# Low parts of table tiles made on VectorE in the gate stage of a decoder layer, and an index row made earlier

## The chip, the cores and the metric

The kernel runs on one core of a Trainium2 chip. What counts is the device time of one execution in microseconds (us), as the median of several runs. The engines are named as in the profile: PE (TensorE, matmuls; PEld its weight loads), DVE (VectorE), ACT (ScalarE), POOL (GpSimd) and SP (SyncE, which issues most DMA transfers). Each engine works through its own queue in order.

## The reference

One layer of a decoder: a norm with scale and shift, a mixer of two attention groups with a residual, a second such norm, and a feed-forward part that picks 16 of 16384 single-neuron experts for each of 8 heads. 512 tokens, width 2048, all in float32. The change touches the last part alone, here shortened:

```python
def peer_ffn(h, w_q, sub_keys, u_tab, v_tab):
    q = (h @ w_q).reshape(B, S, 8, 2, 128)
    s = einsum('bshpd,hpkd->bshpk', q, sub_keys)      # 2 x 128 scores per head
    top_s, top_i = lax.top_k(s, 16)
    cand = top_s[..., 0, :, None] + top_s[..., 1, None, :]
    best_s, best_c = lax.top_k(cand.reshape(..., 256), 16)
    i1 = take_along_axis(top_i[..., 0, :], best_c // 16)
    i2 = take_along_axis(top_i[..., 1, :], best_c % 16)
    expert = i1 * 128 + i2                             # of 128 x 128
    gate = softmax(best_s)
    act = gelu(einsum('td,ted->te', x, u_tab[expert])) # 128 experts per token
    return einsum('te,ted->td', gate * act, v_tab[expert])
```

## The kernel before

The kernel treats 160 tokens sparsely (it gathers rows of the two tables for them by DMA) and the other 352 (`NT`) densely: for these it multiplies with the whole tables u and v and weighs the result with a gate that is zero for experts not picked.

**Products in two parts.** Matmuls with table tiles keep float32 accuracy by splitting both operands. For a half tile of 128 x 1024 weights, `load_w` issues the load of `wraw` on SP, and `split` lets ACT cast it to the high part `whi` (L115) and another engine subtract to get the low part `wlo` (L117); the argument `lo_eng` says which. `whi` and `wlo` have three buffers each, `wraw` has four. `product1(j)` makes one of 128 tiles of u times the tokens: for each of two tile halves 16 matmuls on `whi` (L844) and 8 on `wlo` (L847). It yields between the high and the low part of a half, so that its pieces can be spread among other work. Then ACT takes the gelu (L850). `product2` multiplies with v in the same way (casts L1074, low parts on DVE L1075, matmuls L1080).

**The stages that matter here**, in time: (1) the second stage with the queries, whose weights `w_q` have their low parts on POOL, while DVE picks the top 16; (2) the transposes of the picked indices and gates to `slot` and `gres` (L898 to L906); (3) the gate stage, about 1106 to 1277 us; (4) what is left of the first tiles of u; (5) the long stage of `product2` and further `product1` pieces, with the gathers of the sparse tokens on POOL, to the end.

**The gate stage** builds for each dense token the 128 x 128 table of gates. It runs over 44 groups of 8 tokens. For each group DVE makes four one-hot operations on 128 x 1024 float16: two compares of the index row `iota` with the indices, `o1` (L955) and `o2` (L956), and two products of `o2` with the gates' two parts, `o3` (L960). PE then multiplies `o1` and `o3` token by token (16 table matmuls L967 a group, tile `b_gg`), ACT copies them to `stg` (L970), and SP stores `stg` to DRAM for every 32 tokens. `o1` and `o3` have two buffers, `o2` has one. Between the groups, `next(pieces)` puts one piece of `product1`, so two groups have one tile half between them. 20 tiles of u are made ahead of the fifth stage; 17 of these belong to `product1_pieces`, 34 tile halves, and all have their low parts on POOL.

**The index row** `iota2` is made by POOL (L932), at the head of the gate stage's pool of tiles `ggen`, behind the DMAs of indices and gates (L891, L892) on POOL's queue.

**What follows.** The stored gates come back as `gtile` (four tiles of u at a time, L1051), and `gate()` multiplies the products with them on DVE (L1061), lets ACT cast (L1064) and DVE subtract (L1065). The gathers on POOL (L995) wait for a cast of `product2`.

The order of instructions on each engine is set by a scheduler that goes by the program's order, its dependencies and free buffers; only some are tied by hand (`after`).

## Time and profile before

| what | value |
|---|---|
| median of 3 runs | 3183.56 us (3181.09 to 3184.69) |
| the profiled execution: own time, span | 3180.52 us, 3178.8 us |
| PE busy, share of the span | 3046.1 us, 96% |
| DVE busy | 2585.9 us, 81% |
| ACT busy | 1113.1 us, 35% |
| POOL busy | 937.5 us, 29% |
| low parts on POOL (L117), all forms | x211, 368.7 us |

The times of instructions come from the one profiled execution; the median comes from other runs of the same kernel. A share of busy time is a mean over stages that are limited by different things, so what the change meets is read from its own stage: which engine idles there, and for whom. "Idle before" an instruction is time in which its engine did nothing, and the releaser is what ended it. A matmul's duration overlaps with that of the next; the spacing of their starts tells the pace.

### The profile page before, as it was taken

What the parts mean: (1) busy time and instruction counts of PE and PEld (TensorE: products, weight loads), DVE (VectorE), ACT (ScalarE), POOL (GpSimd) and SP (SyncE); (2) the same over time, 40 slices, a digit from 0 to 9 for tenths busy, and PEclk for the clock granted to TensorE, in tenths of its full rate; (3) what the DMA queues carried; (4) which work ended last, traced back from release to release, by engine and by line L of the source; (5) the groups of instructions that cost most, each with busy time, mean ns of one, the idle gap of its engine ahead of it and who ended that gap; (6) DMA issues with size and microseconds to landing.
All of it is one profiled execution on the core that took longest, in us unless ns stands there. A gap on an engine that the chain in (4) does not pass through costs nothing.

```text
span 3178.8 us, 46249 instructions
## 1 busy us (share of the span) xinstructions
PE 3046.1 (96%) x17617; PEld 2811.5 (88%) x17617; DVE 2585.9 (81%) x3642; ACT 1113.1 (35%) x1604; POOL 937.5 (29%) x630
## 2 busy tenths in 40 slices
PE   3989999999999988999999999999999999999997
PEld 2777777677777877999999999999999999999997
DVE  8988866677589999588888888888888888888885
ACT  3333345432332444433333333333333333333333
POOL 6445430111233433422222222222222222222210
PEclk9999999999999999999999999999999999999999
DMA  7876842148622256899999999999999999999973
GB/s 227 273 237 210 295 157 86 36 145 284 218 93 83 81 193 230 288 339 338 346 332 337 341 340 342 335 351 334 333 348 335 340 336 344 338 346 337 351 297 125
DMA packets 268528, 850.03 MB, mean 267 GB/s; under 512 B 25768, under 2 KB 99528, under 8 KB 224560
## 3 DMA queue, kind: packets, MB, share of 16 engines
q1 hardware_dynamic: 221712, 511.38, 46.8%
q0 software_dynamic: 46592, 335.68, 28.1%
q8 instruction: 138, 2.26, 0.3%
q14 instruction: 86, 0.70, 0.1%
HBM read 814.74 MB, written 32.19 MB: 266 GB/s over the span
## 4 chain that ended last, share of the span: by engine, by line
PE 77%; DVE 15%; DMA 4%; issue 3%; ACT 1%; POOL 0%; SPq 0%; ACTq 0%; DVEq 0%; POOLq 0%
PE b_p L1080 30%; PE b_p L844 19%; PE b_p L847 9%; PE b_o L703 3%; DVE o L960 3%; DMA adaw<-in_ada_w 2%; PE b_pj L109 2%; PE b_pj L110 2%; PE b_pj L108 2%; DVE acc L228 2%; DVE o L955 1%; PE b_o L108 1%; PE b_o L109 1%; PE b_o L110 1%; DVE o L956 1%
## 5 line engine op out<-in xcount | busy, mean ns | idle before, releaser
L115 ACT CAST whi<-wraw 128x1024 fp32r<-128x1024 f32 (+2 forms) x459 | 413.9, 904 | 1032.6 <-PE b_p L844 307.7
L844 PE MATMUL b_p<-h2hi,whi 128*128 128x352 f32 x2048 | 672.4, 329 | 0.0
L844 PE MATMUL b_p<-h2lo,whi 128*128 128x352 f32 x2048 | 667.2, 326 | 0.0
L1080 PE MATMUL b_p<-h2hi,whi 128*128 128x352 f32 x2048 | 655.3, 323 | 1.5 <-DVE xo L1092 0.8
L1080 PE MATMUL b_p<-h2lo,whi 128*128 128x352 f32 x2048 | 653.8, 322 | 0.0
L117 POOL TENSOR_TENSOR wlo<-wraw,whi 128x512 fp32r<-128x512 f32 (+3 forms) x211 | 368.7, 1755 | 460.9 <-ACT whi L115 333.6
L1074 ACT CAST whi<-wraw 128x1024 fp32r<-128x1024 f32 x256 | 268.6, 1049 | 642.8 <-PE b_p L1080 317.3
L1075 DVE TENSOR_TENSOR wlo<-wraw,whi 128x1024 fp32r<-128x1024 f32 x256 | 313.3, 1225 | 161.6 <-ACT whi L1074 138.3
L844 PEld LDWEIGHTS b_p<-h2lo,whi 128*128 128x128 f32 x2048 | 386.6, 189 | 0.1
L844 PEld LDWEIGHTS b_p<-h2hi,whi 128*128 128x128 f32 x2048 | 386.4, 189 | 0.1
L1080 PEld LDWEIGHTS b_p<-h2hi,whi 128*128 128x128 f32 x2048 | 384.4, 188 | 2.4 <-DVE xo L1092 1.1
L1080 PEld LDWEIGHTS b_p<-h2lo,whi 128*128 128x128 f32 x2048 | 384.9, 188 | 0.0
L228 DVE SCALAR_TENSOR_TENSOR acc<-adaw,cact,acc 128x512 f32<-128x512 f32 (+1 forms) x390 | 357.5, 936 | 29.4 <-DMA adaw<-in_ada_w 23.8
L847 PE MATMUL b_p<-h2hi,wlo 128*128 128x352 f32 x2048 | 377.6, 327 | 0.6 <-POOL wlo L117 0.6
L1080 PE MATMUL b_p<-h2hi,wlo 128*128 128x352 f32 x2048 | 369.7, 322 | 0.0
L117 DVE TENSOR_TENSOR wlo<-wraw,whi 128x1024 fp32r<-128x1024 f32 x248 | 304.3, 1227 | 56.0 <-ACT whi L115 53.2
L995 POOL DMA_INDIRECT gat<-in_u_rows,eidx x128 | 195.7, 1529 | 502.8 <-ACT whi L1074 192.2
L847 PEld LDWEIGHTS b_p<-h2hi,wlo 128*128 128x128 f32 x2048 | 339.1, 188 | 0.9 <-POOL wlo L117 0.9
L995 POOL DMA_INDIRECT gat<-in_v_rows,eidx x128 | 185.8, 1451 | 515.7 <-ACT whi L1074 245.2
L1080 PEld LDWEIGHTS b_p<-h2hi,wlo 128*128 128x128 f32 x2048 | 334.0, 188 | 0.0
L1014 DVE SCALAR_TENSOR_TENSOR h2sb<-gat,wt,h2sb 128x2048 f32<-128x2048 f32 x127 | 298.3, 2349 | 24.8 <-DMA gat<-in_v_rows,eidx 24.2
L1001 DVE SCALAR_TENSOR_TENSOR gat<-gat,h2s 128x2048 f32<-128x2048 f32 x128 | 290.8, 2287 | 18.9 <-DMA gat<-in_u_rows,eidx 18.8
(375 smaller groups left out, 4264.5 us busy)
## 6 DMA issues: line engine op xcount, KB each, us to landing
wraw<-in_u_t SPq DMA_DIRECT2D x256, 512.0 KB
wraw<-in_v_t SPq DMA_DIRECT2D x256, 512.0 KB
adaw<-in_ada_w SPq DMA_DIRECT2D x288, 256.0 KB
adaw<-in_ada_w SPq DMA_DIRECT2D x128, 192.0 KB
gd<-stg SPq DMA_DIRECT2D x11, 2048.0 KB
gtile<-gd SPq DMA_DIRECT2D x32, 704.0 KB
wraw<-in_w_out SPq DMA_DIRECT2D x32, 512.0 KB
wraw<-in_w_q SPq DMA_DIRECT2D x32, 512.0 KB
```

The source lines that it names most:

```text
L108: mm(o, wh, xh, start=first, stop=False)
L115: nc.scalar.copy(out=hi, in_=src)
L117: last_lo[0] = e.tensor_tensor(out=lo, in0=src, in1=hi, op=OP.subtract).ins.name
L228: nc.vector.scalar_tensor_tensor(out=acc, in0=w[:, j, :], scalar=cact[:, k:k + 1], in1=acc, op0=OP.mult, op1=OP.add)
L844: mm(b3, uh[:, kk, :], x[:, GA:, k0 + kk, :], start=k0 + kk == 0 and x is h2[0], stop=False)
L847: mm(b3, ul[:, kk, :], h2[0][:, GA:, k0 + kk, :], start=False, stop=k0 + kk == KD - 1)
L995: ins = nc.gpsimd.indirect_dma_start(out=g, out_offset=None, in_=a[table], in_offset=bass.IndirectOffsetOnAxis(ap=idx[:, c:c + 1], axis=0))
L1001: after(nc.vector.scalar_tensor_tensor(out=g, in0=g, scalar=1.0, in1=of(s, h2s, h2sb)[0], op0=OP.mult, op1=OP.mult, accum_out=act0[:, s:s ...
L1014: ins = nc.vector.scalar_tensor_tensor(out=acc, in0=g, scalar=wt0[:, s:s + 1], in1=acc, op0=OP.mult, op1=OP.add)
L1074: pace[0] = nc.scalar.copy(out=vh, in_=vr).ins.name
L1075: pace[1] = nc.vector.tensor_tensor(out=vl, in0=vr, in1=vh, op=OP.subtract).ins.name
L1080: mm(banks[dc][:, :NT], part[:, jj, dc * P:(dc + 1) * P], x, start=first and jj == 0 and part is vh and x is wpair[pair * 2 + jj][0], stop ...
```

## The change

`product1_pieces` asks for its low parts from "vector" instead of "gpsimd": 34 subtractions of 128 x 1024 move from POOL to DVE. And the index row moves out of the pool `ggen` to the pool `slp`, beside the tile `slot`, and is written ahead of the transposes.

```diff
     slot = slp.tile([P, 4, NT], F16, name="slot")
+    iota2 = slp.tile([P, P, 2], F16, name="iota")
+    nc.gpsimd.iota(iota2, pattern=[[1, P], [0, 2]], base=0, channel_multiplier=0,
+                   allow_small_or_imprecise_dtypes=True)
     gres = slp.tile([P, NT], F32, name="gres")
...
     shp = [P, OB // 2, P, 2]
-    iota2 = gg.tile([P, P, 2], F16, name="iota", bufs=1)
-    nc.gpsimd.iota(iota2, pattern=[[1, P], [0, 2]], base=0, channel_multiplier=0,
-                   allow_small_or_imprecise_dtypes=True)
     iota = iota2.unsqueeze(1).broadcast_to(shp)
...
         while done1[0] < RAW + NHOST:
-            yield from product1(next(todo1), "gpsimd")
+            yield from product1(next(todo1), "vector")
             done1[0] += 1
```

Three lines are added ahead of the gate stage and three taken away in it, so lines from L895 to L933 have a number three higher in the changed kernel than before.

Where the instructions go, in the order in which they stand on their engines. A number behind a tile's name tells one buffer's use from another.

DVE at the start of the gate stage, before:

```order
L888 COPY gate0_5825<-gates_7457 128x128
L955 TENSOR_TENSOR o1_9663<-iota_9596,slot_9495 128x1024
L956 TENSOR_TENSOR o2_9664<-iota_9596,slot_9495 128x1024
L905 CAST slot_9495<-gres_9496 128x352
L955 TENSOR_TENSOR o1_9714<-iota_9596,slot_9495 128x1024
L906 TENSOR_TENSOR slot_9495<-gres_9496,slot_9495 128x352
L960 TENSOR_TENSOR o3_9667<-o2_9664,slot_9495 128x1024
L960 TENSOR_TENSOR o3_9669<-o2_9664,slot_9495 128x1024
```

and now:

```order
L888 COPY gate0_5825<-gates_7457 128x128
L955 TENSOR_TENSOR o1_9663<-iota_9496,slot_9495 128x1024
L956 TENSOR_TENSOR o2_9664<-iota_9496,slot_9495 128x1024
L908 CAST slot_9495<-gres_9498 128x352
L117 TENSOR_TENSOR wlo_9604<-wraw_9601,whi_9603 128x1024
L909 TENSOR_TENSOR slot_9495<-gres_9498,slot_9495 128x352
L960 TENSOR_TENSOR o3_9667<-o2_9664,slot_9495 128x1024
L117 TENSOR_TENSOR wlo_9634<-wraw_9631,whi_9633 128x1024
L960 TENSOR_TENSOR o3_9669<-o2_9664,slot_9495 128x1024
```

Two low parts now stand among the first products, and the compare of the second group has gone behind them.

POOL at the same place and to the end of stage 4, a piece of the difference (- before, + now):

```order
 L891 DMA eidxb<-eflat 32x32
 L892 DMA gateb<-gates 32x32
-L932 IOTA iota 128x256
-L117 TENSOR_TENSOR wlo<-wraw,whi 128x1024 x27
 L987 MEMSET accb 128x2048
-L117 TENSOR_TENSOR wlo<-wraw,whi 128x1024 x7
 L995 DMA gat<-in_u_rows,eidxb 128x2048 x16
```

POOL now has nothing between the index DMAs and the gathers but the memset; the index row stands 33 low parts earlier, behind the small index row of the second stage (L760).

DVE in the middle of the gate stage, before:

```order
L956 TENSOR_TENSOR o2_10372<-iota_9596,slot_9495 128x1024
L955 TENSOR_TENSOR o1_10371<-iota_9596,slot_9495 128x1024
L960 TENSOR_TENSOR o3_10375<-o2_10372,slot_9495 128x1024
L960 TENSOR_TENSOR o3_10377<-o2_10372,slot_9495 128x1024
L956 TENSOR_TENSOR o2_10424<-iota_9596,slot_9495 128x1024
L960 TENSOR_TENSOR o3_10427<-o2_10424,slot_9495 128x1024
L955 TENSOR_TENSOR o1_10423<-iota_9596,slot_9495 128x1024
L960 TENSOR_TENSOR o3_10429<-o2_10424,slot_9495 128x1024
```

and now:

```order
L955 TENSOR_TENSOR o1_10371<-iota_9496,slot_9495 128x1024
L956 TENSOR_TENSOR o2_10372<-iota_9496,slot_9495 128x1024
L960 TENSOR_TENSOR o3_10375<-o2_10372,slot_9495 128x1024
L960 TENSOR_TENSOR o3_10377<-o2_10372,slot_9495 128x1024
L955 TENSOR_TENSOR o1_10423<-iota_9496,slot_9495 128x1024
L956 TENSOR_TENSOR o2_10424<-iota_9496,slot_9495 128x1024
L117 TENSOR_TENSOR wlo_10582<-wraw_10579,whi_10581 128x1024
L960 TENSOR_TENSOR o3_10427<-o2_10424,slot_9495 128x1024
L960 TENSOR_TENSOR o3_10429<-o2_10424,slot_9495 128x1024
```

Every second group has a low part between its compares and its products. On PE, around the same place, where the order is that of before:

```order
L847 MATMUL b_p1_10222<-h2hi_7290,wlo_10312 128x352 x8
L967 LDWEIGHTS o1_10371
L967 MATMUL b_gg_10379<-o3_10375,o1_10371 128x128
L967 LDWEIGHTS o1_10371
L967 MATMUL b_gg_10379<-o3_10377,o1_10371 128x128
```

The matmuls on the low part `wlo_10312`, three uses of the buffers before `wlo_10582`, stand ahead of the table matmuls of group 10371.

DVE after the last group of the gate stage, now (before, the gate multiplications followed the last product without a low part among them):

```order
L960 TENSOR_TENSOR o3_11583<-o2_11578,slot_9495 128x1024
L117 TENSOR_TENSOR wlo_11691<-wraw_11688,whi_11690 128x1024
L117 TENSOR_TENSOR wlo_11721<-wraw_11718,whi_11720 128x1024
L117 TENSOR_TENSOR wlo_11754<-wraw_11751,whi_11753 128x1024
L117 TENSOR_TENSOR wlo_11784<-wraw_11781,whi_11783 128x1024
L1061 TENSOR_TENSOR xo_7449<-xo_7449,gtile_12001 128x352
L117 TENSOR_TENSOR wlo_11817<-wraw_11814,whi_11816 128x1024
L1065 TENSOR_TENSOR h2lo_7291<-xo_7449,h2hi_7290 128x352
L1061 TENSOR_TENSOR xo_7449<-xo_7449,gtile_12001 128x352 x3
L1065 TENSOR_TENSOR h2lo_7291<-xo_7449,h2hi_7290 128x352
L1061 TENSOR_TENSOR xo_7449<-xo_7449,gtile_12003 128x352
L117 TENSOR_TENSOR wlo_11847<-wraw_11844,whi_11846 128x1024
```

Four low parts stand ahead of the first gate multiplication and six among those that follow.

## Rows read from the trace of the kernel before

**Rows 1.** Page, part 4: the chain's shares of the span by engine.

```profile
PE 77%; DVE 15%; DMA 4%; issue 3%; ACT 1%; POOL 0%; SPq 0%; ACTq 0%; DVEq 0%; POOLq 0%
```

**Rows 2.** Windows: start:end, length, busy us (x instructions) per engine, PEclk, DMA, GB/s.

```profile
1122.00:1127.00 5.00, 5.00 (x25) 5.00 (x24) 4.58 (x7) 1.20 (x2) 0.00 (x0) 0.54 0.00 0
1143.00:1259.00 116.00, 101.87 (x896) 91.05 (x894) 113.29 (x128) 55.12 (x88) 46.80 (x17) 1.00 0.62 225
1277.00:1321.00 44.00, 43.41 (x275) 43.02 (x274) 20.60 (x28) 20.81 (x32) 29.05 (x12) 1.00 0.78 249
1350.00:1400.00 50.00, 50.00 (x314) 50.00 (x314) 42.75 (x47) 17.85 (x24) 11.89 (x10) 1.00 0.92 339
```

**Rows 3.** Timeline of DVE, mid-stage: start, us, instruction, count [idle before <-releaser].

```profile
1150.30 2.69 DVE L960 TENSOR_TENSOR o<-o,slot 128x1024 f16<-128x1024 f16 x1
1152.91 0.68 DVE L955 TENSOR_TENSOR o<-iota,slot 128x1024 f16<-128x1024 f16 x1
1153.51 0.68 DVE L960 TENSOR_TENSOR o<-o,slot 128x1024 f16<-128x1024 f16 x1
...
1157.55 2.70 DVE L960 TENSOR_TENSOR o<-o,slot 128x1024 f16<-128x1024 f16 x1
```

**Rows 4.** Timeline of POOL at the same time.

```profile
1149.50 2.93 POOL L117 TENSOR_TENSOR wlo<-wraw,whi 128x1024 fp32r<-128x1024 f32 x1 [4.32 <-PE b_p L847]
```

**Rows 5.** Chain of waits, 1260 to 1285: start, us, engine, tile, line, count.

```profile
1271.71 0.94 PE b_gg L967 x16
1272.64 2.68 PE b_p L844 x16
...
1276.25 1.36 PE b_p L847 x8
```

**Rows 6.** Groups by form, 1106 to 1276: count, busy us, mean ns, idle before.

```profile
L117 POOL TENSOR_TENSOR wlo<-wraw,whi 128x1024 fp32r<-128x1024 f32 x24 | 67.1, 2804 | 88.2 <-PE b_p L847 83.9 <-ACT stg L970 4.3
```

**Rows 7.** Timeline of DVE after the stage: a low part, and what follows.

```profile
1329.11 1.23 DVE L1075 TENSOR_TENSOR wlo<-wraw,whi 128x1024 fp32r<-128x1024 f32 x1 [1.91 <-PE b_p L1080]
1330.26 2.28 DVE L1001 SCALAR_TENSOR_TENSOR gat<-gat,h2sb 128x2048 f32<-128x2048 f32 x1
```

**Rows 8.** Timeline of POOL at the stage's start.

```profile
1104.54 1.54 POOL L932 IOTA iota<- 128x256 f16 x1
1106.03 9.39 POOL L117 TENSOR_TENSOR wlo<-wraw,whi 128x1024 fp32r<-128x1024 f32 x4
1116.46 2.34 POOL L117 TENSOR_TENSOR wlo<-wraw,whi 128x1024 fp32r<-128x1024 f32 x1 [1.04 <-PE b_p L847]
```

**Rows 9.** Timeline of DVE at the stage's start.

```profile
1106.11 9.86 DVE L955 TENSOR_TENSOR o<-iota,slot 128x1024 f16<-128x1024 f16 x1 [4.97 <-POOL iota L932]
...
1116.50 2.50 DVE L905 CAST slot<-gres 128x352 f16<-128x352 f32 x1
```

**Rows 10.** Timeline of ACT at the stage's start.

```profile
1104.64 0.28 ACT L902 ACTIVATE gres<-b_sk 128x128 f32<-128x128 f32 x1
```

**Rows 11.** Timeline of PE at the stage's start.

```profile
1115.84 0.49 PE L847 MATMUL b_p<-h2hi,wlo 128*128 128x352 f32 x2
...
1121.29 1.76 PE L967 MATMUL b_gg<-o,o 128*128 128x128 f16 x15 [0.31 <-DVE o L960]
...
1123.25 0.49 PE L844 MATMUL b_p<-h2lo,whi 128*128 128x352 f32 x1
1123.54 0.49 PE L844 MATMUL b_p<-h2hi,whi 128*128 128x352 f32 x1
```

**Rows 12.** Timeline of PE after the stage, low-part matmuls L847.

```profile
1299.34 1.47 PE L847 MATMUL b_p<-h2hi,wlo 128*128 128x352 f32 x8
...
1308.00 1.58 PE L847 MATMUL b_p<-h2hi,wlo 128*128 128x352 f32 x8 [0.58 <-POOL wlo L117]
```

**Rows 13.** Timeline of DVE after the stage, the first gate multiplications.

```profile
1295.14 1.40 DVE L1061 TENSOR_TENSOR xo<-xo,gtile 128x352 f32<-128x352 f32 x3 [21.49 <-DMA gtile<-gd]
```

**Rows 14.** Timeline of POOL in the second stage, behind the sixteen-wide index row.

```profile
896.52 4.71 POOL L117 TENSOR_TENSOR wlo<-wraw,whi 128x1024 fp32r<-128x1024 f32 x2 [4.88 <-ACT whi L115]
```

## The prediction, made before the changed kernel ran

> **What bounds the kernel now.** I read the chain of waits first. It runs over PE for 77% of the span, so nearly everywhere only less idle time on PE pays; DVE has 15% [rows 1]. Then the windows by stage, to find where PE idles: in 1350 to 1400 us, after the gate stage, PE is busy for 50.00 of 50 us, while in 1143 to 1259, the middle of the gate stage, it is busy for 101.87 of 116 and DVE for 113.29 [rows 2]. So in the gate stage DVE sets the pace, and the reader is to see why in DVE's timeline beside POOL's. One period (two groups of 8 tokens) has eight one-hot operations and lasts 1157.55 - 1150.30 = 7.25 us. Seven of them follow each other after 0.6 to 0.8 us; the one that starts at 1150.30 takes 2.69 and the next starts 2.61 later [rows 3]. At that moment POOL makes a low part, from 1149.50 to 1152.43 [rows 4]. There are 17 such low parts in 1143 to 1259 [rows 2] and 17 such long operations on DVE, one in each period, never two and never without POOL. The trace thus shows DVE held until POOL is done. The hold is 2.61 less the usual 0.60 [rows 3] = 2.01 us.
>
> PE's own need in a period is seen at the end of the stage, where the chain runs over PE: 0.94 for each of two groups of table matmuls, 2.68 for the high part of a tile half and 1.36 for its low part, 5.92 us [rows 5]. So PE waits 1.33 us in each period of 7.25.
>
> **The steady part of the stage.** Of the 34 low parts that change engine, 24 lie in the gate stage [rows 6]; five of them come in a heap at the start [rows 8], which leaves 19 in the steady part. What each costs DVE: a low part of the same shape on DVE takes 1.23 us, and the next operation starts 1330.26 - 1329.11 = 1.15 later [rows 7]; I take 1.15, since it is the same instruction between the same engines' work, with 1.40 as the upper bound (a seam of 0.1 to 0.2 on both sides, as between some one-hot operations in [rows 3]). The hold of 2.01 goes, since POOL then has nothing left in the stage but its queue of gathers behind the memset. A period becomes 7.25 - 2.01 + 1.15 = 6.39, still above PE's 5.92, so DVE stays the bound and all of it counts: 19 x 0.86 = **16.3 us**. With 1.40 it is 11.6.
>
> Does a low part make DVE wait? It writes one of three buffers, so it needs the low-part matmuls of the tile half three before. In the order, the low part 10582 stands behind the products 10375 and 10377; the matmuls that free its buffer, those on 10312 (10404 and 10490 have the two other buffers), stand on PE in front of the table matmuls that wait for these very products. When PE waits for DVE, they are long done. The operand whi is cast by ACT, busy for 55.12 of 116 us in that stretch [rows 2]; POOL today starts its low part when PE releases the buffer, not when ACT delivers [rows 4]. I price the wait at nothing.
>
> **The start of the stage.** Today DVE waits 4.97 us for the index row [rows 9], made on POOL from 1104.54 after the index DMAs [rows 8]; then four low parts run on POOL in a row, 9.39 us, and DVE's first compare takes 9.86; the cast behind it takes 2.50, beside the fifth low part [rows 8, 9]. PE has done what stands in front of its first table matmuls at 1115.84 + 0.49 = 1116.3 and gets going at 1121.29 [rows 11]. After the change the index row is long there, and two compares run before ACT delivers the gates at 1104.64 + 0.28 = 1104.9 [rows 10]. Behind that stand the cast, a low part, a subtraction, a product, a low part, a product: 0.5 + 1.15 + 0.5 + 0.6 + 1.15 + 0.6 = 4.5, done at 1109.4 (the cast alone isn't in the trace; between 0.3, half the 0.68 of a compare, and its 2.50 [rows 9], I take 0.5, near to the compares, which have more elements; even 2.50 gives 1111.4). PE then runs from 1116.3 without a pause: 1121.3 - 1116.3 = **5.0 us**. The pause also has a price behind it: in 1122 to 1127, after PE had stood still, the granted clock is 0.54, near the lower of its two levels, 1.2 of 2.4 GHz [rows 2], and matmuls start 0.29 us apart [rows 11] where the same block later takes 2.68 / 16 = 0.17 [rows 5]. 13 of them are so spaced, 13 x 0.12 = **1.6 us**, which should go. Bounds for the two: 3 us, if PE waits for the second group, and 6.6 whole.
>
> **The index row** moves past 33 low parts on POOL's queue, to a place in front of the second stage's low parts, and takes 1.54 us there [rows 8]. POOL sits idle there for 4.88 us before its next low part [rows 14], which waits for ACT; it is hidden, price nothing. Without that cover it would delay one low part by 1.5.
>
> **After the gate stage** ten low parts move. Today PE waits 0.58 us for one of POOL's at 1308.00 [rows 12]: **0.6 us**. In exchange six of the ten stand on DVE behind gate multiplications (L1061) that wait for the gate tiles; the first lands at 1295.14 [rows 13], 19 us after the last table matmuls, which end at 1276.25 [rows 5]. Four low parts stand ahead of them, enough for four tile halves; the fifth is needed by PE at 1299.3 [rows 12] and would be done at 1295.1 + 0.5 + 1.15 = 1296.8. 2.5 us to spare, price nothing; DVE is busy for only 20.60 of 44 us there [rows 2]. The gathers that are now next in POOL's queue wait for ACT's first cast of the following stage, as today, so they don't come forward into this stretch by more than some us.
>
> **The sum** is 16.3 + 5.0 + 1.6 + 0.6 = 23.5 us against the profiled execution's 3180.52 (span 3178.8, with 1.7 around it that nothing touches): 3157.0. The median of the runs stands 3.04 above that execution, so the forecast for the median is 3183.56 - 23.5 = **3160.1 us**. What comes behind is bound by PE at 50.00 of 50 us [rows 2], so a gain made here should stay.
>
> **Rival 1, PE becomes the bound.** If DVE gets ahead at the start and stays there, the stage lasts what PE needs: from 1116.3, 44 groups of 0.94 and 22 tile halves of 4.04 [rows 5] are 130.2 us, to 1246.5 instead of 1276.25. That is 29.7 + 0.6 = 30.3 us: 3153.3. For it: DVE has the first two groups done before PE wants them. Against it: 6.39 against 5.92 in each period. Chance 0.13.
>
> **Rival 2, given back after the stage.** If the gate tiles land later against the end of the stage than today (their stores and loads share the queues with weights), low parts 5 to 10 are late by what exceeds 2.5 us, and PE waits. To leave less than 6 us of gain the landing must slip by 20 us. Against it: the order of the DMA issues is the same in both kernels and the share of the DMA engines is 0.78 there [rows 2]. Chance 0.07 for a result within 0.2%, about 3180.
>
> **Rival 3, slower: the low part waits in DVE's queue.** If a low part reached the head before its buffer is free, the period would be a circle: table matmuls 0.94, high part 2.68, 0.94, low part on PE 1.36, its making on DVE 1.15, two products 1.2, together 8.3 us against 7.25. 19 x 1.0 more, less the 7.2 of start and end: 3195. It decides where PE's low-part matmuls on the freed buffer stands behind the table matmuls that wait for products queued after the low part; the order has it ahead, by one group. Chance 0.03.
>
> **Rival 4, slower: DVE simply has more to do.** If the long operations are not POOL's doing, nothing goes away and each of 19 periods grows by 1.15, 21.9 us, less the 5.0 of the index row: about 3200. Against it: 17 long operations beside 17 low parts, and the 9.86 beside four. Chance 0.04. The Trainium skill, "Perfetto Trace Analysis", section "Optimizing Scalar/DVE Operations", says that offloading from a saturated DVE, even to GpSimd, may make sense; this change does the reverse on a DVE that is busy for 113.29 of 116 us, so by that rule alone one lands here. The same section adds that the two share a read port and that offloading between them might not help; the rows above bear out this half.
>
> **How the numbers follow.** The forecast has 0.73, rival 1 0.13, rival 2 0.07, rivals 3 and 4 together 0.07. Low end: rival 1, and 1 us for the scatter of the runs, 3152. High end: 11.6 + 3 in place of 16.3 + 6.6, no 0.6, gives 3169; with 1 us of scatter, 3170. About 0.2% (6 us) is what can be told from no change here. Faster 0.86, within it 0.07, slower 0.07.
>
> **What would show it.** In the trace of after: no POOL low part after 1103 us, no one-hot operation over 1 us, periods of about 6.4 us on DVE with a low part of 1.2 in each; PE's first table matmuls at about 1116 and the granted clock of the next 5 us near 1; the last table matmuls about 1253 instead of 1276; no PE wait over 1 us for a low part between there and the next stage. Periods of 8 with DVE waiting for PE in front of a low part show rival 3, periods above 8 with long one-hot operations rival 4, and a PE that waits for DVE's low parts after the stage rival 2.

## The result and the profile after

The kernel after takes 3150.86 us in the median of four runs (3147.20 to 3154.82), the kernel before 3182.32 on the same chip; the ratio is 0.9897, with a 95% interval of 0.9880 to 0.9913. The gain of 31 us is larger than the forecast's 23.5 and larger than the 30.3 of its first rival; the time lies 1.1 us under the low end of the range.

The profiled execution of after took 3154.82 us (span 3153.1), which is 25.7 less than that of before. It understates the gain, since something ahead of the stage differs between executions: in all profiles of this study the copy of the first gates (DVE, L888), the last step ahead of the gate stage, starts somewhere between 1097 and 1110 us. In before it starts at 1100.92, in after at 1106.56. The difference of 5.64 us is there before the moved index row can play a part: the small index row of the second stage (L760), which in both kernels stands ahead of it, starts at 891.34 and 896.98, and from there to the copy it is 209.58 us in both. All stage lengths below are therefore counted from that copy; first its line in before, then in after, and the end of the last table matmuls in after (chain of waits; the end in before is in [rows 5]):

```profile
1100.92 0.23 DVE L888 COPY gate<-gates 128x128 f32<-128x128 f32 x1
```

```profile
1106.56 0.23 DVE L888 COPY gate<-gates 128x128 f32<-128x128 f32 x1
```

```profile
1251.32 0.93 PE b_gg L967 x16
1252.25 1.36 PE b_p L847 x8
```

To the end of the last table matmul it is 1276.25 - 1100.92 = 175.33 us in before and 1252.25 - 1106.56 = 145.69 in after: 29.64 less. From there to the end of the span it is 1902.55 and 1900.85: 1.7 less. Together 31.3, close to the 31.5 between the medians.

The page's chain of waits, by engine (answers to [rows 1]):

```profile
PE 84%; DVE 10%; DMA 2%; issue 2%; ACT 1%; SPq 0%; POOL 0%; ACTq 0%; DVEq 0%; POOLq 0%
```

Windows of after, with the columns of [rows 2]: the start of the table matmuls, mid-stage, and the 45 us behind the stage.

```profile
1122.00:1127.00 5.00, 5.00 (x52) 4.87 (x52) 4.10 (x6) 2.81 (x5) 0.00 (x0) 1.00 0.37 131
1143.00:1230.00 87.00, 86.87 (x817) 81.71 (x816) 86.44 (x130) 49.19 (x81) 0.00 (x0) 1.00 0.74 266
1255.00:1300.00 45.00, 45.00 (x284) 45.00 (x283) 27.23 (x40) 21.93 (x32) 3.81 (x3) 1.00 0.95 301
```

PE is now busy for 86.87 of 87 us in the middle of the stage, where it was 101.87 of 116. DVE is as full as before, 86.44 of 87. POOL does nothing. Where the table matmuls start the granted clock is 1.00, the upper of its two levels (2.4 GHz), where it was 0.54.

Timeline of DVE in after, one period and what follows (answers to [rows 3]); the low part L117 has taken the place of the long operation:

```profile
1199.88 0.68 DVE L956 TENSOR_TENSOR o<-iota,slot 128x1024 f16<-128x1024 f16 x1
1200.48 1.22 DVE L117 TENSOR_TENSOR wlo<-wraw,whi 128x1024 fp32r<-128x1024 f32 x1
1201.62 1.28 DVE L960 TENSOR_TENSOR o<-o,slot 128x1024 f16<-128x1024 f16 x2
1202.83 0.68 DVE L955 TENSOR_TENSOR o<-iota,slot 128x1024 f16<-128x1024 f16 x1
1203.43 0.68 DVE L956 TENSOR_TENSOR o<-iota,slot 128x1024 f16<-128x1024 f16 x1
1204.14 1.29 DVE L960 TENSOR_TENSOR o<-o,slot 128x1024 f16<-128x1024 f16 x2
1205.35 0.68 DVE L955 TENSOR_TENSOR o<-iota,slot 128x1024 f16<-128x1024 f16 x1
1205.96 0.68 DVE L956 TENSOR_TENSOR o<-iota,slot 128x1024 f16<-128x1024 f16 x1
```

The period is 1205.96 - 1199.88 = 6.08 us, not 6.39. The eight one-hot operations start 0.60 apart, the low part takes 1.14 of the row (1201.62 - 1200.48), and there is a single wait of 0.11 (1203.43 to 1204.14 is 0.71 instead of 0.60), in front of a product that reads what the compare before it has just written.

The chain of waits of after shows who sets the pace. Columns: start, us, engine, tile, line, count:

```profile
1169.25 0.94 PE b_gg L967 x16
1170.19 2.67 PE b_p L844 x16
1172.85 0.94 PE b_gg L967 x16
1173.79 1.36 PE b_p L847 x8
1175.15 0.99 PE b_gg L967 x16
...
1187.17 0.07 PE b_gg L967
1187.25 0.02 issue
1187.27 1.02 PE b_gg L967 x15
```

Up to 1181 us the blocks of PE follow each other without a gap, 1175.15 - 1169.25 = 5.90 us a period. From there on each second group of table matmuls has a first matmul that stands alone, and the group takes 0.07 + 0.02 + 1.02 = 1.11 us instead of 0.94: PE has caught up with DVE and goes at DVE's 6.08. That lasts to about 1230 us, eight periods; for the last 22 us the chain runs over PE without a pause again. The two engines are almost level.

At the start DVE makes its two compares at once and then waits for ACT's gates; the cast alone takes 0.34 us. PE's first table matmuls follow its own work directly, with no wait (answers to [rows 9] and [rows 11]):

```profile
1106.70 0.68 DVE L955 TENSOR_TENSOR o<-iota,slot 128x1024 f16<-128x1024 f16 x1
1107.30 0.68 DVE L956 TENSOR_TENSOR o<-iota,slot 128x1024 f16<-128x1024 f16 x1
1110.60 0.34 DVE L908 CAST slot<-gres 128x352 f16<-128x352 f32 x1 [2.62 <-ACT gres L905]
...
1121.94 1.09 PE L967 MATMUL b_gg<-o,o 128*128 128x128 f16 x16
```

### The profile page after: what moved, and what is told of

Its sections match the earlier page's. It is cut to its first block, busy times and chain, and to the rows that moved or that the text cites. A ratio compares the mean times of both kernels' runs of the same rounds, so it can differ in the third digit from the quotient of the medians.

```text
span 3153.1 us, 46222 instructions
## 1 busy us (share of the span) xinstructions
PE 3037.6 (96%) x17617; PEld 2808.5 (89%) x17617; DVE 2563.7 (81%) x3676; ACT 1111.5 (35%) x1604; POOL 835.0 (26%) x596
## 3 DMA queue, kind: packets, MB, share of 16 engines
q8 instruction: 138, 2.26, 0.3%
## 4 chain that ended last, share of the span: by engine, by line
PE 84%; DVE 10%; DMA 2%; issue 2%; ACT 1%; SPq 0%; POOL 0%; ACTq 0%; DVEq 0%; POOLq 0%
PE b_p L1080 31%; PE b_p L844 21%; PE b_p L847 10%; PE b_o L703 3%; PE b_pj L109 2%; PE b_pj L110 2%; PE b_pj L108 2%; DVE acc L228 2%; PE b_gg L967 1%; DMA adaw<-in_ada_w 1%; PE b_o L108 1%; PE b_o L109 1%; PE b_o L110 1%; DVE oh L820 1%; PE b_sc L560 1%
## 5 line engine op out<-in xcount | busy, mean ns | idle before, releaser
L1075 DVE TENSOR_TENSOR wlo<-wraw,whi 128x1024 fp32r<-128x1024 f32 x256 | 312.7, 1223 | 159.6 <-ACT whi L1074 130.0
L117 DVE TENSOR_TENSOR wlo<-wraw,whi 128x1024 fp32r<-128x1024 f32 x282 | 345.0, 1224 | 65.1 <-ACT whi L115 62.0
L847 PE MATMUL b_p<-h2hi,wlo 128*128 128x352 f32 x2048 | 377.9, 327 | 0.0
L117 POOL TENSOR_TENSOR wlo<-wraw,whi 128x512 fp32r<-128x512 f32 (+4 forms) x177 | 277.6, 1576 | 344.5 <-ACT whi L115 333.4
L847 PEld LDWEIGHTS b_p<-h2hi,wlo 128*128 128x128 f32 x2048 | 339.1, 188 | 0.0
L995 POOL DMA_INDIRECT gat<-in_u_rows,eidx x128 | 188.3, 1471 | 510.5 <-ACT whi L1074 201.6
```

The source lines that it names most:

```text
L117: last_lo[0] = e.tensor_tensor(out=lo, in0=src, in1=hi, op=OP.subtract).ins.name
L847: mm(b3, ul[:, kk, :], h2[0][:, GA:, k0 + kk, :], start=False, stop=k0 + kk == KD - 1)
L995: ins = nc.gpsimd.indirect_dma_start(out=g, out_offset=None, in_=a[table], in_offset=bass.IndirectOffsetOnAxis(ap=idx[:, c:c + 1], axis=0))
L1075: pace[1] = nc.vector.tensor_tensor(out=vl, in0=vr, in1=vh, op=OP.subtract).ins.name
```

## The experiments

Two questions were open: which of the two edits does what at the start, and why the steady part gave 22 us instead of 16.3. For each kernel the table has the median time, the stage's length from the gate copy to the last table matmul, its part from the first table matmul on, and the usual period of DVE (eight one-hot operations and whatever low part stands between).

| kernel | median us | stage us | from the first table matmul | period |
|---|---|---|---|---|
| before | 3182.32 | 175.33 | 155.56 | 7.26 |
| after | 3150.86 | 145.69 | 130.31 | 6.08 |
| index row alone | 3178.32 | 170.89 | 155.65 | 7.26 |
| low parts alone | 3148.61 | 146.68 | 130.42 | 6.08 |
| before, DVE's order of after | 3180.68 | 174.53 | 157.57 | 7.26 |
| before, o2 in two buffers | 3184.08 | 173.01 | 155.78 | 7.26 |
| after, DVE's order of before | 3152.28 | 147.55 | 132.32 | 6.27 |
| after, o2 in two buffers | 3156.75 | 145.81 | 128.45 | 5.95 |
| no low parts | 3146.33 | 143.78 | 128.47 | 5.89 |
| low parts in turns | 3165.11 | 158.66 | 143.44 | 8.27 and 5.25 |
| after, idle POOL operation | 3203.64 | 195.06 | 179.95 | 8.1 to 8.5 |

The kernel before ran beside them again, with medians of 3182.22, 3185.02 and 3183.46 us. The times carry the scatter of some 10 us that arises ahead of the stage; the columns on the stage don't, and what is said below rests on them.

**The index row alone.** The low parts stay on POOL.

```diff
-            yield from product1(next(todo1), "vector")
+            yield from product1(next(todo1), "gpsimd")
```

> The low parts stay on GpSimd as in the kernel before; only the index row moves. The stage is measured from the end of the gate copy (L888) to the last table matmul, 175.33 us in the profile of before and 145.69 in that of after. Theory A (the start term has a part that belongs to the index row alone: with the row made early, the two compares run before GpSimd's first low part is released, so the first products are done before PE gets through the high parts): 4 to 7 us less in the first 25 us of the stage, nothing in the steady part, which keeps its period of about 7.25; stage 168 to 171 us, time about 3177. Rival B (the start is held by the four low parts on GpSimd, whatever the index row does): stage within 1 us of 175.3, time about 3182.

Measured: 3178.32, ratio 0.9988 (0.9977 to 0.9998), stage 4.44 us shorter, all of it ahead of the first table matmul. Theory A holds. PE's clock in its start shows something else, in the 6 us around the first table matmuls:

```profile
1122.14:1128.14 6.00, 5.62 (x55) 5.15 (x54) 5.79 (x7) 3.58 (x7) 2.83 (x1) 1.00 0.54 174
```

The clock is at 1.00 here too, and yet the part from the first table matmul on is 155.65, as in before with 0.54. Where DVE sets the pace a faster PE gains nothing; the 1.6 us that the prediction counted for the clock need the other edit.

**The low parts alone.** The index row goes back to its old place.

```diff
-    iota2 = slp.tile([P, P, 2], F16, name="iota")
...
+    iota2 = gg.tile([P, P, 2], F16, name="iota", bufs=1)
+    nc.gpsimd.iota(iota2, pattern=[[1, P], [0, 2]], base=0, channel_multiplier=0,
+                   allow_small_or_imprecise_dtypes=True)
```

> The low parts of the gate stage go to VectorE; the index row stays at its old place, behind the transposes. Theory A (with no low parts in front of it, GpSimd makes the row in 1.5 us as soon as its tile's room is free, and the first products are still done before PE has finished the 64 high-part matmuls ahead of them): equal to after, stage 145.7 within 1.5 us, time 3151 within 3. Rival B (the two edits gain side by side, as the prediction's separate terms would have it): about 5 us of the start are missing, stage about 151, time about 3156.

Measured: 3148.61, ratio 0.9903 (0.9886 to 0.9919), stage 146.68. Theory A holds: without POOL's low parts in front of it the late index row costs nothing on the way to the end. Of the 0.99 us by which the stage is longer than in after, 0.88 lie ahead of the first table matmul, where PE has no wait; its clock rose later there, 0.84 in the 6 us in which after has 1.00 (1106.36 is 9.00 behind the gate copy, as is 1115.56 in after):

```profile
1106.36:1112.36 6.00, 6.00 (x33) 6.00 (x33) 6.00 (x8) 1.05 (x1) 0.00 (x0) 0.84 0.61 201
```

So the edits overlap: 4.4 us for the index row alone, 28.7 for the low parts alone, 29.6 together. Beside the low parts on VectorE the index row's move has no effect that these runs show.

**Before, with DVE's operations in the order of after.** Each one-hot operation is tied behind the one written ahead of it, without a semaphore.

```diff
+            def in_row(ins):
+                after(ins, row[0], ORDER)
+                row[0] = ins.ins.name
-            nc.vector.tensor_tensor(out=o1, in0=iota, in1=per_token(0), op=OP.is_equal)
-            nc.vector.tensor_tensor(out=o2, in0=iota, in1=per_token(1), op=OP.is_equal)
+            in_row(nc.vector.tensor_tensor(out=o1, in0=iota, in1=per_token(0), op=OP.is_equal))
+            in_row(nc.vector.tensor_tensor(out=o2, in0=iota, in1=per_token(1), op=OP.is_equal))
...
-                nc.vector.tensor_tensor(out=o3, in0=o2, in1=per_token(2 + n), op=OP.mult)
+                in_row(nc.vector.tensor_tensor(out=o3, in0=o2, in1=per_token(2 + n), op=OP.mult))
```

> The kernel before with one thing changed: VectorE's one-hot operations are held to the order o1 compare, o2 compare, product, product in each group of eight tokens, as they mostly stand in after; low parts stay on GpSimd. In before the scheduler had put the o2 compare of the next group right behind the products that free its buffer, and the products right behind the compare that makes their input. Theory A (the extra gain of the steady part, 22.4 us against the 16.3 of the sum, is idle time between dependent operations on VectorE, 0.43 us per period, that the new order hides): period from 7.25 to about 6.9, stage about 6 us shorter, 169 us, time about 3176. Rival B (the order does not matter; the extra gain comes from GpSimd's port hold being longer than the 2.01 us counted): stage within 1 us of 175.3, time about 3182.

Measured: 3180.68, ratio 0.9999 (0.9987 to 1.0011), the period 7.26 as in before. Theory A, mine, fell. The timelines of DVE and POOL say why (L959 is here the compare o1, L960 the compare o2, L964 the products):

```profile
1187.03 0.69 DVE L960 TENSOR_TENSOR o<-iota,slot 128x1024 f16<-128x1024 f16 x1
1187.75 1.29 DVE L964 TENSOR_TENSOR o<-o,slot 128x1024 f16<-128x1024 f16 x2
1188.96 0.69 DVE L959 TENSOR_TENSOR o<-iota,slot 128x1024 f16<-128x1024 f16 x1
1189.56 2.88 DVE L960 TENSOR_TENSOR o<-iota,slot 128x1024 f16<-128x1024 f16 x1
1192.47 1.29 DVE L964 TENSOR_TENSOR o<-o,slot 128x1024 f16<-128x1024 f16 x2
...
1189.08 2.81 POOL L117 TENSOR_TENSOR wlo<-wraw,whi 128x1024 fp32r<-128x1024 f32 x1 [4.45 <-PE b_p L847]
```

The operation that POOL holds up now takes 1192.47 - 1189.56 = 2.91 to the next, not 2.61. Behind it follows a product that reads its result, and in the group without POOL 0.72 lie between the same two (1187.03 to 1187.75), 0.12 over the usual 0.60; the hold itself is 2.91 - 0.72 = 2.19. In before the held operation is itself a product behind the compare that it reads, and between the starts of the two lie 0.79 us, 0.19 more than the usual 0.60:

```profile
1185.82 0.69 DVE L956 TENSOR_TENSOR o<-iota,slot 128x1024 f16<-128x1024 f16 x1
1186.61 2.69 DVE L960 TENSOR_TENSOR o<-o,slot 128x1024 f16<-128x1024 f16 x1
1189.23 0.68 DVE L955 TENSOR_TENSOR o<-iota,slot 128x1024 f16<-128x1024 f16 x1
```

The hold of 2.01 that I had read was what of a hold of 2.20 falls behind a wait that DVE has anyway. A wait that lies beside POOL's operation costs nothing in before, and taking it away gave nothing.

**Before, with two buffers for o2.**

```diff
-            o2 = gg.tile(shp, F16, name="o2", tag="o2", bufs=1)
+            o2 = gg.tile(shp, F16, name="o2", tag="o2")
```

> The kernel before with a second buffer for the o2 one-hot tile (two small tiles of the id stage change their pool to make room); low parts stay on GpSimd. In before each o2 compare follows products that read the only buffer, with 0.71 us of idle time at that place. Theory A (idle time between dependent operations counts in the pace): the o2 compare can run earlier, period shorter by 0.2 to 0.4 us, stage 4 to 8 us shorter than 175.3, time about 3176. Rival B (the idle time is only where the port hold shows, and moves elsewhere): stage within 1 us of 175.3, time about 3182.

Measured: 3184.08, ratio 0.9993 (0.9982 to 1.0004), period 7.26: rival B as to the pace. (The 0.71 us that the expectation calls idle time is the distance between two starts; 0.11 of it is a wait.) The stage is 2.3 us shorter, more than rival B allows, but all of that and more lies ahead of the first table matmul; from there on it is 155.78. DVE and POOL, one period:

```profile
1192.92 0.69 DVE L956 TENSOR_TENSOR o<-iota,slot 128x1024 f16<-128x1024 f16 x1
1193.53 2.88 DVE L960 TENSOR_TENSOR o<-o,slot 128x1024 f16<-128x1024 f16 x1
1196.34 0.68 DVE L955 TENSOR_TENSOR o<-iota,slot 128x1024 f16<-128x1024 f16 x1
...
1192.93 2.94 POOL L117 TENSOR_TENSOR wlo<-wraw,whi 128x1024 fp32r<-128x1024 f32 x1 [4.32 <-PE b_p L847]
```

The held product now starts 0.61 behind the compare, without the extra 0.19, and is held for 1196.34 - 1193.53 - 0.60 = 2.21 instead of 2.01. This is the same hold of 2.2 us for the third time, with and without a wait inside it.

**After, with DVE's operations in the order of before** (o2, product, o1, product in one group; o2, o1, product, product in the next), tied in the same way.

```diff
+            if t8 % 2:
+                in_row(nc.vector.tensor_tensor(out=o2, in0=iota, in1=per_token(1), op=OP.is_equal))
+                in_row(nc.vector.tensor_tensor(out=o1, in0=iota, in1=per_token(0), op=OP.is_equal))
+            else:
+                in_row(nc.vector.tensor_tensor(out=o2, in0=iota, in1=per_token(1), op=OP.is_equal))
...
+                if t8 % 2 == 0 and n == 0:
+                    in_row(nc.vector.tensor_tensor(out=o1, in0=iota, in1=per_token(0), op=OP.is_equal))
```

> The kernel after with one thing changed: VectorE's one-hot operations are held to the order that they have in the kernel before (o2, product, o1, product in one group, o2, o1, product, product in the next); low parts on VectorE. Theory A (order hides idle time between dependent operations): period 6.2 to 6.4 instead of 5.9 to 6.08, stage 3 to 6 us longer than 145.7, time 3154 to 3157. Rival B (order does not matter): stage within 1 us of 145.7, time about 3151.

Measured: 3152.28, ratio 0.9914 (0.9897 to 0.9931), stage 147.55, 1.9 us longer than after; period 6.27. Here the order does count: with POOL silent, no hold covers the waits between dependent operations. Theory A has the period right and the stage a little too long. It forgot PE: the period is 0.2 longer, over 19 periods 3.7 us, but half of after's periods were set by PE's 5.90 and not by DVE, so that not all of it counts. The medians of the two kernels can't be told apart; the reading rests on the period. On DVE (L960 and L963 are o2, L961 and L970 o1, L967 products):

```profile
1180.89 1.22 DVE L117 TENSOR_TENSOR wlo<-wraw,whi 128x1024 fp32r<-128x1024 f32 x1
1182.03 0.69 DVE L963 TENSOR_TENSOR o<-iota,slot 128x1024 f16<-128x1024 f16 x1
1182.82 0.69 DVE L967 TENSOR_TENSOR o<-o,slot 128x1024 f16<-128x1024 f16 x1
1183.43 0.69 DVE L970 TENSOR_TENSOR o<-iota,slot 128x1024 f16<-128x1024 f16 x1
1184.03 0.68 DVE L967 TENSOR_TENSOR o<-o,slot 128x1024 f16<-128x1024 f16 x1
1184.75 0.69 DVE L960 TENSOR_TENSOR o<-iota,slot 128x1024 f16<-128x1024 f16 x1
```

Two waits are left: 0.19 from a compare to the product behind it (1182.03 to 1182.82) and 0.12 from a product to the compare that takes the buffer (1184.03 to 1184.75). A third, which before has between the second group's products and the next compare, is covered by the low part that stands there.

**No low parts in the stage.** Left out is the making of the low parts of these 17 tiles; the tile matmuls read the high part in their place, so that PE does as much.

```diff
+        if lo_eng == "none":
+            nc.scalar.copy(out=hi, in_=src)
+            return hi, hi
```

> The kernel after with the low parts of the gate stage left out: no engine makes them, and the tile matmuls that would read them read the high part again, so PE's work is the same count of matmuls (part left out: the low-order half of the first product of the tiles made in this stage). Theory A (in after PE and VectorE are almost level, PE at 5.90 us per period and VectorE at 6.07): only PE's pace is left, 0.17 us less in about 9 of 19 periods, stage 1 to 3 us shorter than 145.7, that is 143 to 145, time about 3149. Rival B (VectorE still sets the pace of the steady part by itself, as the sum had it): each low part taken away gives back its 1.14 us, 19 x 1.14 = 22 us, stage about 124, time about 3129.

Measured: 3146.33, ratio 0.9882 (0.9861 to 0.9903), stage 143.78, 1.9 us shorter than after. Theory A holds: PE alone needs 5.89 a period, and a seventh less work for DVE (21.7 of some 145 us) moves almost nothing. What DVE has left over it now spends waiting for PE to free the buffers of the products. Groups by line on DVE, with the idle time in front and its releaser (L963 are here the products, L970 the table matmuls):

```profile
L963 DVE TENSOR_TENSOR o<-o,slot 128x1024 f16<-128x1024 f16 x88 | 58.6, 686 | 22.8 <-PE b_gg L970 22.8
```

The wait is 22.8 us, about the 19 x 1.14 = 21.7 that the low parts took in the steady part.

**Low parts in turns**: the first half of each tile of u on POOL, the second on DVE.

```diff
-            uh, ul = load_w(ws, a["u_t"][j][:, k0:k0 + 8, :], [P, 8, P], lo_eng)
+            uh, ul = load_w(ws, a["u_t"][j][:, k0:k0 + 8, :], [P, 8, P], "gpsimd" if lo_eng == "turns" and k0 == 0 else "vector" if lo_eng == "turns" else lo_eng)
```

> The kernel after with every second low part of the gate stage (the first half of each table tile) given back to GpSimd. Theory A (the price of a low part on GpSimd is the time for which VectorE stands still beside it, about 2.0 us, against 1.14 on VectorE, and PE's pace of 5.90 is met in the other periods): about 9 or 10 periods of 6.8 to 7.25, the rest 5.9 to 6.1; stage about 155, halfway between 175 and 146 or a little under, time 3160 to 3165. Rival B (with half the low parts on each side neither engine is the bound, and the load is balanced): stage at or under 145.7, time 3151 or less.

Measured: 3165.11, ratio 0.9938 (0.9921 to 0.9955), stage 158.66. Theory A holds in the main, though its 155 for the stage was too short; from the first table matmul on it is 143.44, and the middle between before and after is 142.9. Two periods together take 8.27 + 5.25 = 13.52, which is 2 x 6.76 (counted from another operation of the eight they are 7.24 and 6.28, with the same sum). Sharing the work between the two engines doesn't balance it: a held compare takes 2.67 to the next start (1195.72 to 1198.39 in DVE's timeline), so DVE stands 2.07 us for each low part that POOL makes, 2.19 with a wait of 0.12 in front of it, and spends 1.14 on each that it makes itself.

**After, with an operation on POOL that nobody waits for.**

```diff
+        if lo_eng == "both" and spares[0] is not None:
+            spare = spares[0].tile([P, 4, P], F16, name="spare", tag="spare", bufs=1)
+            for h in range(2):
+                nc.gpsimd.tensor_tensor(out=spare, in0=src[:, 4 * h:4 * h + 4], in1=hi[:, 4 * h:4 * h + 4], op=OP.subtract)
```

> The kernel after, with GpSimd also subtracting the same two tiles, in two halves, into a scratch tile that nobody reads. Nothing waits for the result. Theory A (VectorE is held while GpSimd runs such an operation, whoever needs it): each period grows by the hold, about 1.5 to 2.0 us for the 2.4 to 2.9 us on GpSimd, less the little that PE is ahead; stage longer by 25 to 38 us, 171 to 184, time 3176 to 3189. Rival B (in before the low part cost time since its result came late, not since it held VectorE): no change, stage 145.7 within 1, time about 3151.

Measured: 3203.64, 52.8 us over after and ratio 1.0051 (1.0031 to 1.0070) to before; stage 195.06, 49.4 us longer than after. Rival B falls: no result of POOL is awaited, and yet DVE stands. Its lost time isn't idle time behind another engine either: between the first and the last table matmul the trace shows only 0.5 us in which DVE waited for another engine. Theory A has the mechanism, and its upper end of 38 us was too low, since it counted 19 periods and at most 2.0 us in each. With 22 tile halves between the first and the last table matmul the stage grew by (179.95 - 130.31) / 22 = 2.26 for each. That is counted from after's stage, in which PE sets half of the periods; DVE's own period grew from 6.08 to 8.3 in the mean, by 2.2. DVE and POOL (L961 and L962 compares, L966 products, L122 the idle subtraction):

```profile
1189.65 1.77 DVE L962 TENSOR_TENSOR o<-iota,slot 128x1024 f16<-128x1024 f16 x1
1191.46 2.24 DVE L966 TENSOR_TENSOR o<-o,slot 128x1024 f16<-128x1024 f16 x2
1193.62 0.68 DVE L961 TENSOR_TENSOR o<-iota,slot 128x1024 f16<-128x1024 f16 x1
...
1189.49 3.05 POOL L122 TENSOR_TENSOR spare<-wraw,whi 128x512 f16<-128x512 f32 x2 [3.86 <-issue]
```

Each half-size operation on POOL stretches one one-hot operation: the compare takes 1.81 to the next start instead of 0.60, the pair of products 2.16 instead of 1.21. That is 1.21 + 0.95 = 2.16 for both.

**After, with two buffers for o2**, the same edit as on before.

> The kernel after with a second buffer for the o2 one-hot tile (the same two small tiles of the id stage change their pool as in the run on the kernel before). In after VectorE's period of 6.07 us is eight one-hot operations at 0.60, a low part at 1.14 and one wait of 0.11 between an operation and the one that reads its result; PE's pace alone is 5.90 (the run without low parts, stage 143.78). Theory A (what VectorE loses between dependent operations counts as soon as nothing else holds it, so that the two engines meet if it goes): period at most 5.97, stage 143.8 to 145.2, less than 2 us below after and so hardly to be told from it by time, about 3149 to 3150. Rival B (with o2 written ahead the scheduler's order puts the waits elsewhere, as in the kernel before): period 6.07 to 6.3, stage 145.7 to 148.

Measured: 3156.75 (3146.71 to 3158.60), ratio 0.9904 (0.9872 to 0.9936). The period is 5.95 = 8 x 0.60 + 1.14, with no wait left, and the part from the first table matmul on is 128.45, PE's own 128.47. Theory A holds for the pace. One period on DVE, from low part to low part:

```profile
1199.16 1.26 DVE L117 TENSOR_TENSOR wlo<-wraw,whi 128x1024 fp32r<-128x1024 f32 x1
1200.30 0.72 DVE L955 TENSOR_TENSOR o<-iota,slot 128x1024 f16<-128x1024 f16 x1
...
1204.51 0.72 DVE L960 TENSOR_TENSOR o<-o,slot 128x1024 f16<-128x1024 f16 x1
1205.11 1.26 DVE L117 TENSOR_TENSOR wlo<-wraw,whi 128x1024 fp32r<-128x1024 f32 x1
```

For the stage theory A does not hold: it is 145.81, since the first table matmul came 2.0 us later than in after. This seems to be a price of the edit itself. ACT's copy L925 waits 1.09 us for a DMA that reads `eflat`, one of the two small tiles that the edit moves:

```profile
1114.97 1.57 ACT L925 COPY h2sb<-b_pj 128x512 f32<-128x512 f32 x3 [1.09 <-DMA eidxb<-eflat]
```

PE stands idle for 0.94 us behind that copy, and its clock rises later (0.76 in the 6 us from 9 us behind the gate copy, 1.00 in after). The run with the same edit on before has the same wait (0.77); neither before nor after has it. By time the kernel can't be told from after, and no version that clearly beats after came out of these runs; a second buffer for o2 without that wait wasn't tried.

## Why the prediction came out as it did

The direction and the mechanism of the hold were right; the size was too small by 8 us, of which 6.1 are the steady part's, and the range was missed by 1.1 us. That margin says little: single runs of after lie between 3147.20 and 3154.82, and the range allowed 1 us for scatter. What failed is seen in the trace. Term by term:

- **What bounds the kernel before** was right: DVE, held by POOL's low parts. The idle operation on POOL shows that the hold needs no data dependence, and the other three kernels with all of POOL's low parts keep the period of 7.26. (Of the 17 long operations that the prediction counts, 16 begin inside 1143 to 1259 us and the last one at 1259.24.)
- **The start**, 5.0 us: from the gate copy to the full run of table matmuls it was 1121.29 - 1100.92 = 20.37 and is 1121.94 - 1106.56 = 15.38, 4.99 less. The first pair of products was foreseen for 1109.4; it is done at 1114.88, less the 5.64 by which this stage began later 1109.2. The sum gave the 5.0 to both edits together; it didn't foresee that either edit alone brings most of it.
- **The clock**, 1.6 us: the granted clock is 1.00 in place of 0.54 as foreseen. The index row alone showed that this is worth something only because the low parts leave DVE at the same time. The first table matmuls themselves, also at the low clock in before, gave 0.6 more that wasn't counted (16 of them to the next block: 1122.81 - 1121.29 = 1.52 for the last 15, 0.90 for all 16 in after).
- **The steady part**, 16.3 us foreseen, 22.4 measured (29.64 - 4.99 - 1.6 - 0.6). This is the step that failed: "A period becomes 7.25 - 2.01 + 1.15 = 6.39, still above PE's 5.92, so DVE stays the bound and all of it counts". The period became 6.08, and PE's 5.90 set the pace for the first ten periods. The low part's 1.15 was right (1.14). The subtraction was not: it left in the period the 0.4 us of waits between dependent operations that stood in before, as if they were part of the eight operations' cost. With 8 x 0.60 = 4.83 for the operations (0.604 each), before is 4.83 + a hold of 2.20 + two waits of together 0.24; after is 4.83 + 1.14 + one wait of 0.11. The difference is 1.18 a period, and 19 x 1.18 = 22.4. That this meets the measured 22.4 so exactly is in part luck: ten of after's periods went at PE's 5.90, which gains more than 1.18 each, while in before, too, the first two periods ran over PE in the chain of waits, up to 1135.56, and gained less. Two runs split the 0.31 by which 6.39 was too long: in the order of before the period is 6.27, so 0.12 is a wait that the low part covers by standing in it; the other 0.19, from 6.27 to 6.08, is the scheduler's new order, in which a compare or the low part stands between an operation and the one that reads its result. The order of the changed kernel's instructions was there to be read before the run, and the sum should have been made along it, row by row.
- **Rival 1, PE becomes the bound**, had 0.13, against it "6.39 against 5.92 in each period". With 6.08 against 5.90 that objection was nearly gone. Its sum, the stage from 1116.3 on at PE's pace, 130.2 us, came out at 130.31, and its 29.7 for the stage at 29.64. So close a match is luck: between 44 groups there is room for 22 high and 21 low parts, so the sum has a low part of 1.36 too many, and PE's own pace, as the run without low parts shows, is 128.47. PE sets the pace for the first ten periods and DVE by a hair for most of the rest; without any low part the stage is 1.9 us shorter, so that is all that DVE still costs.
- **After the stage**, 0.6 foreseen, 1.7 measured: PE's wait of 0.58 at 1308.00 [rows 12] is gone, and PE is busy for all 45.00 us behind the stage, which rules out rival 2. What made the other 1.1 wasn't tried; in the three other kernels of the study that kept all low parts on POOL this stretch took 1902.0 to 1904.1, in the five that kept none 1900.2 to 1901.4.
- **Rivals 3 and 4** fell by the timeline: DVE waits for PE in front of a low part only once, 0.77 us at 1122.19, and once, 1.04 us at 1118.26, for ACT's cast; both lie at the start, where PE doesn't wait for DVE. No one-hot operation is long. Rival 4's rule, that a saturated DVE may be relieved by GpSimd (the Trainium skill, "Perfetto Trace Analysis", section "Optimizing Scalar/DVE Operations"), is answered by the run in turns: giving half the low parts back to POOL made the stage 13.0 us longer. The section's own caution, that moving work between these two might not help, is what the traces bear out.

## What to carry to other kernels

An operation on POOL that holds VectorE is charged to VectorE at nearly its full length, here 2.2 of 2.34 us against 1.14 for VectorE doing the work itself. Where VectorE paces the stage, as here, compare these two prices before sharing work with POOL; half and half was worse here than all of it on VectorE. When one term of a period goes, add the period up anew from the order that the instructions will have, with the waits between dependent operations as terms of their own: one that falls beside a hold is free, any other counts. And when a bound is lifted to within some per cent of the next engine's pace, that engine's floor is the better forecast than the remainder of a subtraction.

## What the runs showed of the hardware

- POOL's subtraction of 128 x 1024 float32 holds a VectorE operation on float16 for 2.20 us, whichever operation it is (a compare or a product: 2.19, 2.21, and 2.01 + 0.19 or 2.07 + 0.12 where a wait falls into the hold), and one of 128 x 512 with a float16 result for about 1.1. The Trainium skill, "Trainium Architecture — The Big Picture", section "What this means for kernel authors", says that these two engines contend for a shared pair of ports and that it is an exclusive lock, not a division of bandwidth; the rows agree, since a held operation stands for about the length of POOL's and the next ones run at their usual 0.60.
- The hold goes both ways: the same low part on POOL reads 2.93 to 2.95 when it starts together with an operation of VectorE (1192.93, POOL, beside 1192.92, DVE, above), and 2.34 when it starts ahead of one [rows 8, 9]. The difference, 0.6, is one one-hot operation. Where several low parts on POOL follow each other, two things were seen: four in a row held a single compare for 9.86 us [rows 9], while in the run with the index row alone three in a row (8.29 us from 1113.68 on) let VectorE finish one operation beside each (2.69 us from 1114.21 on, then two in 5.68 from 1116.84 on). What decides between the two wasn't tried.
- Two VectorE operations of which the second reads or overwrites what the first has just used start 0.11 to 0.19 us further apart than independent ones (0.19 where the chain of waits also shows a step of DVE's sequencer, DVEq L960, in front of the product). One other operation between them hides it, as the period of 5.95 without any such wait shows.
